# Modulation scale summed on TensorE, shift on VectorE, and the first products taken channel tile by channel tile

## The chip, the cores and the metric

The kernel runs on one core of one Trainium2 chip. The time is that of the device, in microseconds (us), for one launch; the kernel before was run three times, and its median is 2421.31 us. Engines are named as in the profile: PE (TensorE's matmuls), PEld (its weight loads), DVE (VectorE), ACT (ScalarE), POOL (GpSimd) and SP (SyncE, which issues most DMAs).

## The reference

Two transformer blocks on 1024 tokens with 1024 channels. The change lies in the first: a condition vector is turned into shift, scale and gate, the normalised x is modulated by the first two, and a gated delta net (8 key heads, 16 value heads, chunks of 64 tokens) runs on the result.

```
cond = silu(c)
mod = cond @ ada_w[0] + ada_b[0]                       # 1024 -> 3 * 1024
shift, scale, gate = split(mod, 3)
hdn = rms_norm(x, norm_g) * (1.0 + scale) + shift
proj = hdn @ w_in                                      # q, k, v, z, b_lin, a_lin
qkv = silu(causal_depthwise_conv(qkv, conv_w))         # 4 taps
beta = sigmoid(b_lin)
g = -exp(a_log) * softplus(a_lin + dt_bias);  gc = cumsum(g) in each chunk
... delta rule, chunk by chunk: y
x = x + gate * y;  x = rms_norm(x, final_g)
```

The second block (window attention, latent attention and a layer of 16 experts) is not touched.

## The kernel before

All matrices are fp32. A product is made of three matmuls in a reduced fp32 format: each operand is split into a high part (`hi`, a copy by ACT) and a low part (`lo`, the difference, by DVE), and `mm3` adds hi x hi, hi x lo and lo x hi in PSUM (L691 to L693). A matmul takes a weight tile of 128x128 and 512 tokens; a projection of 128 channels (`project`) is 8 channel tiles x 2 halves of the tokens x 3 = 48 matmuls into a PSUM tile of 128x1024 (`psj`). Two such tiles exist (pool `pj`), and they take turns: the third product can start only when the first tile has been read out.

The order of the first block:

- `norm_in` loads x in 8 tiles of 128 tokens (SP's queue). For four tiles at a time, ACT takes the sums of squares (L152), DVE the inverse root in eleven small steps (L154, L34 to L40), ACT normalises (L158), PE transposes (L161, eight 128x128 pieces a tile), and ACT copies into `xT` (L162): channels on partitions, tokens along a row.
- Meanwhile `ada_w` comes in blocks of 128x1024 (512 KB each) through six buffers. `matvec` multiplies each by a column of `cond` and adds it up on DVE (L134, L136), the 8 blocks of the scale first, then the 8 of the shift; PE takes the sums over the partitions against a column of ones (L167), and DVE finishes `mod` and `sc` (L190, L191).
- `modulate` works on halves of 512 tokens: ACT writes `hThi` (L175), DVE and POOL take turns in scaling `xT` in place (L179, L177), and DVE writes `hTlo` (L180).
- `decay` makes the product for beta and g (weights `wbh`, `wbl`), copies it out (`ba`, L239), and goes through a chain of small steps on DVE, ACT and PE (`pba`, `pcs`, `pcr`) to `gr` (L292), which SP stores to DRAM (`gc_d`) and loads again spread out (`D`).
- `gdn` projects K (`yk`), then makes the gate vector in `ada_gate`, with 8 more blocks of `ada_w` (three buffers, SP's queue, behind the store of `gr`), summed on DVE in `accg` and over the partitions on PE (L204); then Q (`yq`), the first two V heads (`yv`), and so on for 8 key heads. `conv_silu` reads a product with ACT (first tap, L221) and DVE (the other three taps, L224), which frees its PSUM tile.

Which instruction follows which on an engine is set by a scheduler from the order of the code; each engine then works through its own list in order, and waits on semaphores for the others. The names that the rows below use: `accg` is the gate's sum, `psm` and `psg` the PSUM tiles of the vectors' partition sums, `pgr` and `ptk` those of the first small products of a key head.

Of the kernel before, what the change touches and what calls it, by code (L numbers as in the profile page):

```python
# [10 lines left out]
F32 = mybir.dt.float32  # L11
# [35 lines left out]
class Net:  # L47
# [20 lines left out]
    def block1(self):  # L68
        nc, a = self.nc, self.a
        with ExitStack() as ps_, ExitStack() as big:  # L70
            self.gc_st = ExitStack()
            self.gc_pool = self.pool(self.gc_st, "g_c", "right")
            pa = self.pool(ps_, "pa", space=PSUM)
            pj = self.pool(big, "pj", "right", PSUM)
            hp = self.pool(big, "hp", "right")
            self.wp = self.pool(big, "g_w", "right")
            hT = [[hp.tile([128, T], F32R, name=f"{n}{k}") for k in range(KT)] for n in ("hThi", "hTlo")]
            with ExitStack() as s0:
                dk = self.pool(s0, "dk", "right")
# [3 lines left out]
                self.decay(hT, pj, pa, dk)  # L83
# [44 lines left out]
    def matvec(self, p, col, acc, bufs, tag="adaw"):  # L128
        nc = self.nc
        for k in range(KT):  # L130
            w = p.tile([128, 1024], F32, tag=tag, name="adaw", bufs=bufs)
            nc.sync.dma_start(w, self.a["ada_w"][0, k * 128:k * 128 + 128, col:col + 1024])
            if k == 0:
                nc.vector.tensor_scalar(acc, w, self.cond[:, 0:1], None, op0=OP.mult)  # L134
            else:
                nc.vector.scalar_tensor_tensor(acc, w, self.cond[:, k:k + 1], acc, op0=OP.mult, op1=OP.add)  # L136

    def norm_in(self, pj, pa, hT, p):
        nc, a = self.nc, self.a
        ident = self.ident  # L140
        acc = [p.tile([128, 1024], F32, name=f"acc{i}") for i in range(2)]
# [5 lines left out]
        sc = p.tile([128, KT], F32, name="sc")  # L147

        def norm(h):
            tiles = range(h * 4, h * 4 + 4)  # L150
            for t in tiles:
                nc.scalar.activation(jk, xs[t], AF.Square, accum_out=ss[:, 0, t:t + 1])  # L152
            s = slice(h * 4, h * 4 + 4)
            nc.vector.tensor_scalar(ss[:, 0, s], ss[:, 0, s], 1.0 / D, EPS, op0=OP.mult, op1=OP.add)  # L154
            rsqrt(nc, p, ss[:, 1, s], ss[:, 0, s], [4])
            for t in tiles:
                x = xs[t]
                nc.scalar.activation(x, x, AF.Copy, scale=ss[:, 1, t:t + 1])  # L158
                pt = pj.tile([128, KT, 128], F32, tag="pj", name="pt", bufs=2)
                for k in range(KT):  # L160
                    nc.tensor.transpose(pt[:, k], x[:, k * 128:(k + 1) * 128], ident)  # L161
                nc.scalar.activation(xT[:, :, t * 128:(t + 1) * 128], pt, AF.Copy)  # L162

        def modulation(i):
            self.matvec(p, i * 1024, acc[i], 6)
            for m in range(8):
                nc.tensor.matmul(ps[:, i * 8 + m:i * 8 + m + 1], lhsT=acc[i][:, m * 128:m * 128 + 128],  # L167
                                 rhs=self.ones[:, 0:1], start=True, stop=True)

        def modulate(h):  # L170
            s = slice(h * 512, h * 512 + 512)
            for k in range(KT):
                sh, sg = mod[:, k:k + 1], sc[:, k:k + 1]
                hi, lo, x = hT[0][k][:, s], hT[1][k][:, s], xT[:, k, s]
                nc.scalar.activation(hi, x, AF.Identity, bias=sh, scale=sg)  # L175
                if k % 2:
                    nc.gpsimd.tensor_scalar(x, x, sg, sh, op0=OP.mult, op1=OP.add)  # L177
                else:
# [12 lines left out]
        nc.vector.scalar_tensor_tensor(sc, mod[:, 8:16], 1.0, self.ngain, op0=OP.add, op1=OP.mult)  # L191
        modulate(0)
        modulate(1)

    def ada_gate(self, pa, p):
        nc, a = self.nc, self.a
        acc = p.tile([128, 1024], F32, tag="y_q", name="accg", bufs=2)
        self.matvec(p, 2048, acc, 3, "y_vz")
        row = p.tile([1, D], F32, tag="y_q", name="grow", bufs=2)
        nc.gpsimd.dma_start(row, a["ada_b"][:, 2048:3072])  # L200
# [27 lines left out]
    def decay(self, hT, pj, pa, q):  # L228
        nc = self.nc
        p = self.gc_pool  # L230
        hi, lo = self.wba
        self.split(hi[:, :, 0:32], lo[:, :, 0:32], self.wbf)
        ps = pj.tile([128, T], F32, tag="pj", name="psj", bufs=2)
        for n in range(2):
            for k in range(KT):
                s = slice(n * 512, (n + 1) * 512)
                self.mm3(ps[:, s], hi[:, k], lo[:, k], hT[0][k][:, s], hT[1][k][:, s], k == 0, k == KT - 1)
# [19 lines left out]
        s = q.tile(S3, F32, name="s")  # L257
# [1354 lines left out]
```

## Time and profile before

| | us |
|---|---|
| runs | 2420.91, 2421.31 (median), 2424.42 |
| profiled execution | 2423.83, of it span 2422.1 |
| PE busy | 2302.6 (95%) |
| DVE busy | 1840.0 (76%) |
| ACT busy | 1387.7 (57%) |
| POOL busy | 160.4 (7%) |

PE is the busiest engine by far. The page's picture of 40 slices of 60 us gives the first of them busy shares of 5 and 8 tenths for PE and nearly all others 9, so what PE can still save lies at the start and in a few slices near 1850 us. The rows further below are from the first 140 us, and one from a later stretch.

### The profile page before, as it was taken

The page shows a single profiled execution, that of the slowest core. Times are in us where ns is not written, and L with a number is a line of the kernel's source. Part 1 is how long each engine was busy: PE and PEld are TensorE (multiplying, and loading weights), DVE is VectorE, ACT ScalarE, POOL GpSimd, SP SyncE. Part 2 cuts the span into 40 slices and gives each one's busy share as a digit, 9 for nine tenths or more (in the row PEclk, how much of TensorE's full clock was granted, in tenths as well). Part 3 has the DMA queues.
Part 4 walks back from the last instruction along what each step waited for, and adds up shares of the span by engine and source line. Part 5 has one row for each costly group of instructions (what it writes and reads, how often), then busy time and mean ns, then how long its engine had stood idle before and what let it go on. Part 6 is the DMA issues. An engine that isn't in the chain of part 4 may idle for free. (4 is left out here: it accounts for less than half of the span.)

```text
span 2422.1 us, 34804 instructions
## 1 busy us (share of the span) xinstructions
PE 2302.6 (95%) x12285; PEld 1884.2 (78%) x12285; DVE 1840.0 (76%) x4307; ACT 1387.7 (57%) x2505; POOL 160.4 (7%) x254
## 2 busy tenths in 40 slices
PE   5899999999999999999999999999976999999998
PEld 4678788888878776777887887887865888888886
DVE  6896778595867854475448978886897898988986
ACT  6344545463544433342437767776434777777775
POOL 2100100001000000000000000000001111111110
PEclk8999999999999999999999989999997999999999
DMA  6422331223222134574412222103347999999993
GB/s 230 147 64 49 79 79 43 77 53 79 62 66 75 32 87 157 171 214 135 76 43 62 72 72 76 30 14 120 119 161 272 370 392 379 385 391 371 381 385 108
DMA packets 262905, 373.99 MB, mean 154 GB/s; under 512 B 90785, under 2 KB 179745, under 8 KB 262730
## 3 DMA queue, kind: packets, MB, share of 16 engines
q1 hardware_dynamic: 217450, 322.51, 39.5%
q10 hardware_dynamic: 39504, 28.15, 4.0%
q0 software_dynamic: 5776, 21.11, 3.2%
q8 instruction: 97, 1.59, 0.3%
q14 instruction: 78, 0.64, 0.1%
HBM read 327.53 MB, written 44.18 MB: 153 GB/s over the span
## 5 line engine op out<-in xcount | busy, mean ns | idle before, releaser
L53 DVE TENSOR_TENSOR whl<-wf,whl 128x2048 fp32r<-128x2048 f32 (+1 forms) x195 | 436.5, 2256 | 55.7 <-ACT whl L52 53.9
L52 ACT ACTIVATE whl<-wf 128x2048 fp32r<-128x2048 f32 (+1 forms) x195 | 368.8, 1895 | 106.4 <-PE psg L693 103.1
L693 PE MATMUL psj<-hThi,wlo 128*128 128x512 f32 x768 | 316.8, 413 | 0.0
L691 PE MATMUL psj<-hThi,whi 128*128 128x512 f32 x768 | 316.5, 412 | 0.0
L692 PE MATMUL psj<-hTlo,whi 128*128 128x512 f32 x768 | 315.4, 411 | 0.0
L692 PE MATMUL psg<-whl,th 128*128 128x512 f32 x768 | 305.1, 397 | 0.0
L693 PE MATMUL psg<-whl,tl 128*128 128x512 f32 x768 | 303.5, 395 | 1.0 <-DVE tl L53 1.0
L691 PE MATMUL psg<-whl,th 128*128 128x512 f32 x768 | 295.5, 400 | 0.0
L52 ACT ACTIVATE whi<-wf 128x512 fp32r<-128x512 f32 (+1 forms) x112 | 77.1, 691 | 184.9 <-PE psj L692 153.4
L693 PEld LDWEIGHTS psg<-whl,tl 128*128 128x128 f32 x768 | 144.9, 189 | 34.5 <-DVE tl L53 1.4
L692 PEld LDWEIGHTS psg<-whl,th 128*128 128x128 f32 x768 | 145.1, 189 | 34.1 <-DVE whl L53 1.6
L691 PEld LDWEIGHTS psg<-whl,th 128*128 128x128 f32 x768 | 144.5, 189 | 32.7 <-ACT th L52 0.6
L692 PEld LDWEIGHTS psj<-hTlo,whi 128*128 128x128 f32 x768 | 146.0, 190 | 24.8
L693 PEld LDWEIGHTS psj<-hThi,wlo 128*128 128x128 f32 x768 | 146.0, 190 | 24.5 <-issue 0.2
L691 PEld LDWEIGHTS psj<-hThi,whi 128*128 128x128 f32 x768 | 145.7, 190 | 24.2
L53 DVE TENSOR_TENSOR wlo<-wf,whi 128x512 fp32r<-128x512 f32 (+1 forms) x112 | 85.1, 762 | 88.8 <-ACT whi L52 87.3
L691 PE MATMUL psy<-whi,ohi 128*128 128x512 f32 x240 | 96.4, 402 | 7.2 <-ACT ohi L52 7.2
L52 ACT ACTIVATE th<-pst 128x512 fp32r<-128x512 f32 x110 | 59.4, 567 | 71.4 <-PE pst L836 42.0
L693 PE MATMUL psy<-whi,olo 128*128 128x512 f32 x240 | 96.4, 402 | 3.6 <-DVE olo L53 3.5
L53 DVE TENSOR_TENSOR pl<-psP,ph 128x512 fp32r<-128x512 f32 x128 | 82.7, 683 | 20.4 <-ACT ph L52 19.4
L692 PE MATMUL psy<-wlo,ohi 128*128 128x512 f32 x240 | 95.7, 399 | 0.0
L52 ACT ACTIVATE ph<-psP 128x512 fp32r<-128x512 f32 x128 | 69.4, 594 | 32.5 <-PE psP L1141 28.5
(447 smaller groups left out, 5196.2 us busy)
## 6 DMA issues: line engine op xcount, KB each, us to landing
wf<-in_w_down_dram SPq DMA_DIRECT2D x64, 1024.0 KB, 7.4
wf<-in_w_gate_dram SPq DMA_DIRECT2D x62, 1024.0 KB, 8.7
wf<-in_w_up_dram SPq DMA_DIRECT2D x62, 1024.0 KB, 9.1
wf<-in_gdn_w_in_dram SPq DMA_DIRECT2D x96, 256.0 KB, 3.0
of<-oT_d ACTq DMA_DIRECT2D x60, 256.0 KB, 3.4
adaw<-in_ada_w_dram SPq DMA_DIRECT2D x24, 512.0 KB, 5.2
D<-gc_d SPq DMA_DIRECT2D x32, 256.0 KB, 3.2
oT_d<-z SPq DMA_DIRECT2D x16, 512.0 KB, 3.0
```

The lines of the kernel that those rows point to most:

```text
L52: self.halved = (self.nc.scalar.activation(hi, src, AF.Copy), self.nc.vector.tensor_sub(lo, src, hi.bitcast(F32)))
L53: self.nc.vector.tensor_sub(lo, src, hi.bitcast(F32)))
L691: nc.tensor.matmul(ps, lhsT=ah, rhs=wh, start=first, stop=False)
L692: nc.tensor.matmul(ps, lhsT=ah, rhs=wl, start=False, stop=False)
L693: nc.tensor.matmul(ps, lhsT=al, rhs=wh, start=False, stop=last)
```

## The change

Four things change in the first block.

- **Vectors.** The blocks of shift and scale come in turn (shift 0, scale 0, shift 1, ...), through seven buffers; the first of each is issued by GpSimd, the others by SP. The shift is summed by DVE as before; for the scale PE multiplies each piece of 128x128 of a block with its column of `cond` (N = 1, 64 products), and DVE adds up the 8 partial sums. The small loads are issued before the norms.
- **Modulation.** It goes by channel tile, all 1024 tokens at once. ACT scales `xT` for tiles 2, 4 and 6, DVE for the others; POOL does nothing here.
- **First products.** `first_products` makes the decay product and the first K product together, channel tile by channel tile, in the two PSUM tiles; `decay` starts from the finished product, and the first `conv_in("k")` takes the finished K.
- **Gate.** The partition sums of `accg` are 8 products with N = 1 into a column, in place of two with N = 512 into a row, and the bias is loaded and the result stored as a column, 4 bytes at a time.

```diff
@@ norm_in
-        def modulation(i):
-            self.matvec(p, i * 1024, acc[i], 6)
-            for m in range(8):
-                nc.tensor.matmul(ps[:, i * 8 + m:i * 8 + m + 1], lhsT=acc[i][:, m * 128:m * 128 + 128],
-                                 rhs=self.ones[:, 0:1], start=True, stop=True)
...
-        def modulate(h):
-            s = slice(h * 512, h * 512 + 512)
-            for k in range(KT):
-                sh, sg = mod[:, k:k + 1], sc[:, k:k + 1]
-                hi, lo, x = hT[0][k][:, s], hT[1][k][:, s], xT[:, k, s]
-                nc.scalar.activation(hi, x, AF.Identity, bias=sh, scale=sg)
-                if k % 2:
-                    nc.gpsimd.tensor_scalar(x, x, sg, sh, op0=OP.mult, op1=OP.add)
-                else:
-                    nc.vector.tensor_scalar(x, x, sg, sh, op0=OP.mult, op1=OP.add)
-                nc.vector.tensor_sub(lo, x, hi.bitcast(F32))
+        def modulate(k):
+            sh, sg = mod[:, k:k + 1], sc[:, k:k + 1]
+            hi, lo, x = hT[0][k], hT[1][k], xT[:, k]
+            nc.scalar.activation(hi, x, AF.Identity, bias=sh, scale=sg)
+            if k in (2, 4, 6):
+                nc.scalar.activation(x, x, AF.Identity, bias=sh, scale=sg)
+            else:
+                nc.vector.tensor_scalar(x, x, sg, sh, op0=OP.mult, op1=OP.add)
+            nc.vector.tensor_sub(lo, x, hi.bitcast(F32))
...
+        blocks = []
+        for k in range(KT):
+            for i in range(2):
+                blocks.append(self.ada_block(p, i * 1024, k, 7, eng=nc.gpsimd if k == 0 else None))
+        self.small_loads()
         norm(0)
-        modulation(1)
-        modulation(0)
-        self.small_loads()
         norm(1)
-        nc.vector.tensor_add(mod, ps[:, 0:16], self.adab)
+        for k in range(KT):
+            self.matvec(blocks[2 * k], k, acc)
+            for m in range(8):
+                nc.tensor.matmul(part[:, m, k:k + 1], lhsT=blocks[2 * k + 1][:, m * 128:m * 128 + 128],
+                                 rhs=self.cond[:, k:k + 1], start=True, stop=True)
+        self.column_sums(ps[:, 0:8], acc)
+        nc.vector.tensor_reduce(mod[:, 8:16], part, axis=AX.X, op=OP.add)
+        nc.vector.tensor_add(mod[:, 8:16], mod[:, 8:16], self.adab[:, 8:16])
         nc.vector.scalar_tensor_tensor(sc, mod[:, 8:16], 1.0, self.ngain, op0=OP.add, op1=OP.mult)
-        modulate(0)
-        modulate(1)
+        nc.vector.tensor_add(mod[:, 0:8], ps[:, 0:8], self.adab[:, 0:8])
+        for k in range(KT):
+            modulate(k)
@@ ada_gate
-        for n in range(2):
-            s = slice(n * 512, n * 512 + 512)
-            ps = pa.tile([128, 512], F32, tag="a", name="psg", bufs=2)
-            nc.tensor.matmul(ps, lhsT=self.ones, rhs=acc[:, s], start=True, stop=True)
-            nc.vector.tensor_add(row[:, s], row[:, s], ps[0:1])
-        nc.sync.dma_start(self.gate_d, row)
+        col = p.tile([128, 8], F32, tag="gcol", name="gcol")
+        nc.sync.dma_start(col, a["ada_b"][:, 2048:3072].rearrange("o (m p) -> p (o m)", p=128))
+        ps = pa.tile([128, 512], F32, tag="a", name="psg", bufs=2)
+        self.column_sums(ps, acc)
+        nc.vector.tensor_add(col, col, ps[:, 0:8])
+        nc.sync.dma_start(self.gate_d.rearrange("o (m p) -> p (o m)", p=128), col)
+    def first_products(self, hT, pj):
+        hi, lo = self.wba
+        self.split(hi[:, :, 0:32], lo[:, :, 0:32], self.wbf)
+        psd, psk = [pj.tile([128, T], F32, tag="pj", name="psj", bufs=2) for i in range(2)]
+        w = [self.load_w(self.wp, self.w_in[:, kk:kk + 4, 1024:1152], [4, 128], bufs=3) for kk in (0, 4)]
+        for k in range(KT):
+            for ps, wh, wl in ((psd, hi[:, k], lo[:, k]), (psk, w[k // 4][0][:, k % 4], w[k // 4][1][:, k % 4])):
+                for n in range(2):
+                    s = slice(n * 512, (n + 1) * 512)
+                    self.mm3(ps[:, s], wh, wl, hT[0][k][:, s], hT[1][k][:, s], k == 0, k == KT - 1)
+        return psd, psk
```

How the lists of the engines move. First PE, from the fourth transposed tile of x to the first product, in the kernel before (`pt` is a tile in transposition, `psm` the vectors' sums):

```order
L161 MATMUL pt_208<-ident_67,x3_143 128x128 x8
L167 MATMUL psm_138<-ones_116,acc1_133 128x1 x8
L161 MATMUL pt_308<-ident_67,x4_144 128x128 x8
L161 MATMUL pt_319<-ident_67,x5_145 128x128 x8
L161 MATMUL pt_330<-ident_67,x6_146 128x128 x8
L161 MATMUL pt_341<-ident_67,x7_147 128x128 x8
L167 MATMUL psm_138<-ones_116,acc0_132 128x1 x8
L691 MATMUL psj_404<-hThi0_87,wbh_123 128x512
```

The four transposed tiles of the second half stand together, between the two sets of column sums. The same place on PE after the change, from the fifth tile of x (`x4`) on:

```order
L168 MATMUL pt_275<-ident_67,x4_143 128x128 x8
L194 MATMUL psm_137<-cond_106,adaw_173 128x1 x7
L168 MATMUL pt_286<-ident_67,x5_144 128x128 x8
L194 MATMUL psm_137<-cond_106,adaw_173 128x1
L168 MATMUL pt_297<-ident_67,x6_145 128x128 x8
L194 MATMUL psm_137<-cond_106,adaw_177 128x1 x8
L168 MATMUL pt_308<-ident_67,x7_146 128x128 x8
L194 MATMUL psm_137<-cond_106,adaw_181 128x1 x8
L194 MATMUL psm_137<-cond_106,adaw_185 128x1 x8
L142 MATMUL psm_137<-ones_116,acc_132 128x1 x8
L705 MATMUL psj_429<-hThi0_87,wbh_123 128x512
```

Products of four blocks of the scale (`adaw_173` to `adaw_185`) now stand among and behind the transposes, and the shift's column sums behind them. Second, PE around `pba`, the first small step of the decay chain on PE, in the kernel before (`wbh`, `wbl` are the decay weights, `whi`, `wlo` those of K):

```order
L691 MATMUL psj<-hThi_94,wbh 128x512
L692 MATMUL psj<-hTlo_102,wbh 128x512
L693 MATMUL psj<-hThi_94,wbl 128x512
L693 MATMUL psj<-hThi_87,wlo 128x512
L691 MATMUL psj<-hThi_87,whi 128x512
L692 MATMUL psj<-hTlo_95,whi 128x512
L693 MATMUL psj<-hThi_87,wlo 128x512
L691 MATMUL psj<-hThi_88,whi 128x512
L242 MATMUL pba<-ident,ba 128x32 x8
```

Here the decay product ends when K has just begun (`hThi_87` and `hThi_94` are the first and the last channel tile). The same place after the change:

```order
L706 MATMUL psj<-hTlo_102,wbh 128x512
L707 MATMUL psj<-hThi_94,wbl 128x512
L705 MATMUL psj<-hThi_94,whi 128x512
L706 MATMUL psj<-hTlo_102,whi 128x512
L707 MATMUL psj<-hThi_94,wlo 128x512
L705 MATMUL psj<-hThi_94,whi 128x512
L706 MATMUL psj<-hTlo_102,whi 128x512
L707 MATMUL psj<-hThi_94,wlo 128x512
L255 MATMUL pba<-ident,ba 128x32 x8
```

The decay product now ends six matmuls before the end of K, and the matmuls behind `pba` are those of Q. Third, DVE from `gr` to the third tap of K after the change (`accg` is the first step on the gate's first block):

```order
L305 COPY gr<-pcr 128x128
L299 TENSOR_TENSOR kdf<-kdf,beta 128x128
L53 TENSOR_TENSOR wlo<-wf,whi 128x512
L244 SCALAR_TENSOR_TENSOR yk<-psj,cw,yk 128x1023
L244 SCALAR_TENSOR_TENSOR yk<-psj,cw,yk 128x1022
L136 TENSOR_SCALAR accg<-adaw,cond 128x1024
L244 SCALAR_TENSOR_TENSOR yk<-psj,cw,yk 128x1021
```

This list reads as before but for its line numbers: the gate's first step stands between the second and the third tap of K.

## Rows read from the trace of the kernel before

**Rows 1.** Windows: busy us of PE, PEld, DVE, ACT, POOL; PEclk; DMA share; GB/s.
```profile
8.00:12.00 4.00, 0.00 (x0) 0.00 (x0) 0.00 (x0) 3.12 (x5) 0.00 (x0) 1.00 1.04 392
...
32.00:36.00 4.00, 3.75 (x18) 3.75 (x19) 3.83 (x7) 3.23 (x3) 0.00 (x0) 0.50 0.88 321
36.00:40.00 4.00, 3.92 (x24) 3.68 (x22) 3.89 (x4) 1.94 (x2) 0.00 (x0) 0.67 0.99 296
...
48.00:52.00 4.00, 4.00 (x10) 2.53 (x10) 3.97 (x7) 4.00 (x6) 3.94 (x3) 0.50 0.00 0
...
sum 140.00, PE 103.61 PEld 81.14 DVE 105.90 ACT 76.36 POOL 24.50; mean PE 2.96 PEld 2.32 DVE 3.03 ACT 2.18 POOL 0.70
...
180.00:220.00 40.00, 40.00 (x294) 33.53 (x293) 21.96 (x71) 17.09 (x58) 5.43 (x20) 1.00 0.24 52
```

**Rows 2.** Timeline, ACT: start, duration, line, operation, [idle before <-releaser].
```profile
11.18 1.06 ACT L152 ACTIVATE jk<-x 128x1024 f32<-128x1024 f32 x1 [0.20 <-DMA x<-in_x_dram]
...
14.74 4.27 ACT L158 ACTIVATE x<-x,ss 128x1024 f32<-128x1024 f32 x4 [1.11 <-DVE ss L40]
...
24.85 1.06 ACT L152 ACTIVATE jk<-x 128x1024 f32<-128x1024 f32 x1
...
32.70 3.23 ACT L158 ACTIVATE x<-x,ss 128x1024 f32<-128x1024 f32 x3 [6.70 <-DVE ss L40]
...
45.02 11.41 ACT L175 ACTIVATE hThi<-xT,mod,sc 128x512 fp32r<-128x512 f32 x16 [1.26 <-DVE sc L191]
...
65.67 1.02 ACT L239 ACTIVATE ba<-psj 32x1024 f32<-32x1024 f32 x1 [7.68 <-PE psj L693]
```

**Rows 3.** Timeline, DVE, from the second inverse root to `sc`.
```profile
26.03 0.17 DVE L154 TENSOR_SCALAR ss<-ss 128x4 f32<-128x4 f32 x1 [2.19 <-ACT jk L152]
...
33.36 9.21 DVE L136 SCALAR_TENSOR_TENSOR acc<-adaw,cond,acc 128x1024 f32<-128x1024 f32 x7
...
44.82 0.17 DVE L191 SCALAR_TENSOR_TENSOR sc<-mod,ng 128x8 f32<-128x8 f32 x1
```

**Rows 4.** Timeline, PE, before the first product.
```profile
32.25 3.57 PE L167 MATMUL psm<-ones,acc 128*128 128x1 f32 x16 [9.57 <-DVE acc L136]
35.69 4.23 PE L161 MATMUL pt<-ident,x 128*128 128x128 f32 x24
...
42.62 1.95 PE L167 MATMUL psm<-ones,acc 128*128 128x1 f32 x16 [0.34 <-DVE acc L136]
```

**Rows 5.** Timeline, DVE, first and last steps of the modulation.
```profile
45.87 0.55 DVE L179 TENSOR_SCALAR xT<-xT,sc,mod 128x512 f32<-128x512 f32 x1 [0.88 <-ACT hThi L175]
...
62.86 1.27 DVE L180 TENSOR_TENSOR hTlo<-xT,hThi 128x512 fp32r<-128x512 f32 x2
```

**Rows 6.** Timeline, PE, from the end of the modulation to V1.
```profile
64.19 0.50 PE L692 MATMUL psj<-hTlo,wbh 128*128 128x512 f32 x1 [2.04 <-DVE hTlo L180]
...
77.92 0.39 PE L691 MATMUL psj<-hThi,whi 128*128 128x512 f32 x1
...
88.82 0.39 PE L691 MATMUL psj<-hThi,whi 128*128 128x512 f32 x1
...
99.13 1.98 PE L204 MATMUL psg<-accg,ones 128*128 128x512 f32 x4 [0.85 <-DVE accg L136]
...
109.31 0.77 PE L691 MATMUL psj<-hThi,whi 128*128 128x512 f32 x1
```

**Rows 7.** Timeline, DVE, from `gr` to the gate's last block.
```profile
77.89 0.28 DVE L292 COPY gr<-pcr 128x128 f32<-128x128 f32 x1
...
83.75 0.75 DVE L134 TENSOR_SCALAR accg<-adaw,cond 128x1024 f32<-128x1024 f32 x1 [1.46 <-DMA adaw<-in_ada_w_dram]
84.42 1.28 DVE L224 SCALAR_TENSOR_TENSOR yk<-psj,cw,yk 128x1021 f32<-128x1021 f32 x1
...
97.79 1.29 DVE L136 SCALAR_TENSOR_TENSOR accg<-adaw,cond,accg 128x1024 f32<-128x1024 f32 x1
```

More of the change, by code (lines that the diff above doesn't have):

```diff
@@ L82, in block1 @@
                     self.norm_in(pj, pa, hT, self.pool(s1, "n1"))
-                self.decay(hT, pj, pa, dk)
+                psd, self.psk = self.first_products(hT, pj)
+                self.decay(psd, pa, dk)
             with ExitStack() as s2:
@@ L126, in small_loads, with ada_block, matvec, column_sums @@
         nc.sync.dma_start(self.nw, a["gdn_norm_w"].rearrange("o (p u) -> (o p) u", u=1))
-    def matvec(self, p, col, acc, bufs, tag="adaw"):
-        nc = self.nc
-        for k in range(KT):
[L131 to L134, printed above, removed]
-            else:
-                nc.vector.scalar_tensor_tensor(acc, w, self.cond[:, k:k + 1], acc, op0=OP.mult, op1=OP.add)
+    def ada_block(self, p, col, k, bufs, tag="adaw", eng=None):
+        w = p.tile([128, 1024], F32, tag=tag, name="adaw", bufs=bufs)
+        (eng or self.nc.sync).dma_start(w, self.a["ada_w"][0, k * 128:k * 128 + 128, col:col + 1024])
+        return w
+    def matvec(self, w, k, acc):
+        if k == 0:
+            self.nc.vector.tensor_scalar(acc, w, self.cond[:, 0:1], None, op0=OP.mult)
+        else:
+            self.nc.vector.scalar_tensor_tensor(acc, w, self.cond[:, k:k + 1], acc, op0=OP.mult, op1=OP.add)
+    def column_sums(self, ps, acc):
+        for m in range(8):
+            self.nc.tensor.matmul(ps[:, m:m + 1], lhsT=acc[:, m * 128:m * 128 + 128], rhs=self.ones[:, 0:1], start=True, stop=True)
     def norm_in(self, pj, pa, hT, p):
@@ L140, in norm_in @@
         ident = self.ident
-        acc = [p.tile([128, 1024], F32, name=f"acc{i}") for i in range(2)]
+        acc = p.tile([128, 1024], F32, name="acc")
         jk = p.tile([128, D], F32, name="jk")
@@ L147, in norm_in @@
         sc = p.tile([128, KT], F32, name="sc")
+        part = ps[:, 64:128].rearrange("p (m k) -> p m k", k=KT)
         def norm(h):
@@ L162, in norm @@
                 nc.scalar.activation(xT[:, :, t * 128:(t + 1) * 128], pt, AF.Copy)
-        def modulation(i):
-            self.matvec(p, i * 1024, acc[i], 6)
-            for m in range(8):
-                nc.tensor.matmul(ps[:, i * 8 + m:i * 8 + m + 1], lhsT=acc[i][:, m * 128:m * 128 + 128],
-                                 rhs=self.ones[:, 0:1], start=True, stop=True)
-        def modulate(h):
-            s = slice(h * 512, h * 512 + 512)
-            for k in range(KT):
-                sh, sg = mod[:, k:k + 1], sc[:, k:k + 1]
-                hi, lo, x = hT[0][k][:, s], hT[1][k][:, s], xT[:, k, s]
-                nc.scalar.activation(hi, x, AF.Identity, bias=sh, scale=sg)
-                if k % 2:
-                    nc.gpsimd.tensor_scalar(x, x, sg, sh, op0=OP.mult, op1=OP.add)
-                else:
-                    nc.vector.tensor_scalar(x, x, sg, sh, op0=OP.mult, op1=OP.add)
-                nc.vector.tensor_sub(lo, x, hi.bitcast(F32))
+        def modulate(k):
[4 more added lines that the diff above has]
+                nc.scalar.activation(x, x, AF.Identity, bias=sh, scale=sg)
+            else:
+                nc.vector.tensor_scalar(x, x, sg, sh, op0=OP.mult, op1=OP.add)
+            nc.vector.tensor_sub(lo, x, hi.bitcast(F32))
         xs = [p.tile([128, D], F32, name=f"x{t}") for t in range(NT)]
@@ L184, in norm_in @@
             nc.sync.dma_start(xs[t], a["x"][0, t * 128:(t + 1) * 128, :])
+        blocks = []
[3 more added lines that the diff above has]
+        self.small_loads()
         norm(0)
-        modulation(1)
-        modulation(0)
-        self.small_loads()
         norm(1)
-        nc.vector.tensor_add(mod, ps[:, 0:16], self.adab)
+        for k in range(KT):
+            self.matvec(blocks[2 * k], k, acc)
+            for m in range(8):
+                nc.tensor.matmul(part[:, m, k:k + 1], lhsT=blocks[2 * k + 1][:, m * 128:m * 128 + 128],
[3 more added lines that the diff above has]
+        nc.vector.tensor_add(mod[:, 8:16], mod[:, 8:16], self.adab[:, 8:16])
         nc.vector.scalar_tensor_tensor(sc, mod[:, 8:16], 1.0, self.ngain, op0=OP.add, op1=OP.mult)
-        modulate(0)
-        modulate(1)
+        nc.vector.tensor_add(mod[:, 0:8], ps[:, 0:8], self.adab[:, 0:8])
+        for k in range(KT):
+            modulate(k)
     def ada_gate(self, pa, p):
@@ L197, in ada_gate @@
         acc = p.tile([128, 1024], F32, tag="y_q", name="accg", bufs=2)
-        self.matvec(p, 2048, acc, 3, "y_vz")
-        row = p.tile([1, D], F32, tag="y_q", name="grow", bufs=2)
-        nc.gpsimd.dma_start(row, a["ada_b"][:, 2048:3072])
-        for n in range(2):
-            s = slice(n * 512, n * 512 + 512)
-            ps = pa.tile([128, 512], F32, tag="a", name="psg", bufs=2)
-            nc.tensor.matmul(ps, lhsT=self.ones, rhs=acc[:, s], start=True, stop=True)
-            nc.vector.tensor_add(row[:, s], row[:, s], ps[0:1])
-        nc.sync.dma_start(self.gate_d, row)
+        for k in range(KT):
+            self.matvec(self.ada_block(p, 2048, k, 3, "y_vz"), k, acc)
+        col = p.tile([128, 8], F32, tag="gcol", name="gcol")
[9 more added lines that the diff above has]
+        w = [self.load_w(self.wp, self.w_in[:, kk:kk + 4, 1024:1152], [4, 128], bufs=3) for kk in (0, 4)]
+        for k in range(KT):
+            for ps, wh, wl in ((psd, hi[:, k], lo[:, k]), (psk, w[k // 4][0][:, k % 4], w[k // 4][1][:, k % 4])):
[3 more added lines that the diff above has]
+        return psd, psk
     def project(self, pj, hT, src):
@@ L226, in conv_silu, with decay @@
         nc.scalar.activation(y, y, AF.Silu)
-    def decay(self, hT, pj, pa, q):
+    def decay(self, ps, pa, q):
         nc = self.nc
         p = self.gc_pool
[L231 to L237, printed above, removed]
         ba = q.tile([32, T], F32, name="ba")
@@ L303, in gdn @@
         ng = getattr(self, "ng", 8)
-        kT = self.conv_in("k", 1024)
+        kT = self.conv_in("k", 1024, ps=self.psk)
         self.ada_gate(pa, p)
@@ L341, in oload_early, with conv_in @@
         return {i: (hi[:, i], lo[:, i]) for i in range(4)}
-    def conv_in(self, nm, col, tag=None, bufs=2):
-        ps = self.project(self.pj, self.hT, self.w_in[:, :, col:col + 128])
+    def conv_in(self, nm, col, tag=None, bufs=2, ps=None):
+        if ps is None:
+            ps = self.project(self.pj, self.hT, self.w_in[:, :, col:col + 128])
         y = self.gp.tile([128, T], F32, tag="y_" + (tag or nm), name="y" + nm, bufs=bufs)
```

## The prediction

> **What bounds the kernel now.** I read the busy time by stretches of 40 us first. From 180 us on PE works 40.00 of 40.00 us at full clock [rows 1]. Nearly all later stretches look like it, so a shift of the moment at which PE becomes saturated is carried to the end, one for one. The change touches only what lies before that: the first 140 us, in which PE is busy for 103.61 us and idle for 36.4 [rows 1]. There the question is what PE waits for. The timeline of the single engines shows it: ACT waits for x to land, DVE sums the modulation vectors, PE transposes, and all of it meets in `sc`, ready at 44.82 + 0.17 = 44.99 us, from which the modulation starts [rows 2 to 4]. I call this moment t0, and the same moment in the changed kernel t0'. A second meeting point lies behind it: PE starts the second V product (V1) at 109.31, t0 + 64.3, after a column of waits that begins with the decay product [rows 6, 7]. So the working has two parts: how far t0 moves, and how far V1 moves against t0.
>
> The profiled execution took 2423.83 us (span 2422.1 and 1.7 around it), 2.5 above the median of the runs, 2421.31. I sum against 2423.83 and take 2.5 off at the end.
>
> **Part 1: the two norms, the vectors, and t0.**
> *Loads.* Two blocks of 512 KB now go out on GpSimd's queue while x is loading. The transfers already move 392 GB/s in that stretch at a DMA share of 1.04 [rows 1], so each block costs whatever shares the engines with it 512 KB / 392 GB/s = 1.34 us. The fourth x tile is needed first: its square begins 0.20 us after it lands, at 11.18 [rows 2]. Bounds of its delay: 0 (the blocks come behind x) and 2.7 us (both ahead of it). I take 2.5, since the second queue starts at the same time as SP's. Then the first normalisation moves from 14.74 to 17.2, and the ACT chain behind it, with the last square (24.85 + 1.06), ends at 28.4 instead of 25.9. The Trainium skill, "DMA: Bandwidth & Descriptors", section "Issuing engines are not separate DMA queues", says that transfers started from sync, scalar and gpsimd run on the same 16 engines and interleave, and that a second issuer saves only issue time. By that rule the delay is real and near 2.7; were the queues apart, it would be 0.
>
> *The second rsqrt.* From 26.03 to 32.70 its eleven small steps took 6.7 us [rows 2, 3], because DVE put a matvec step of about 1.2 us between them four times. With the scale's eight blocks off DVE, one or two come between: 6.7 less 2.4 to 3.6. The second normalisation then starts at 28.5 + 3.1 to 4.3, so at 31.6 to 32.8; I take 32.7, no gain. Without the DMA delay it would be 30.2.
>
> *PE between the norms and t0.* Here the change costs. Its order is strict: four transposed tiles (8 passes each), with the scale's blocks 4 to 7 between and behind them, then the shift's column sums. An fp32 product with one column appears as two passes (16 records for 8 products, rows 4). So behind the second normalisation PE has 4 x 8 + 4 x 16 + 16 = 112 passes, against 32 + 16 before, and before the first 24 transposes already ran while DVE still summed. At the low clock a pass costs (35.69 - 32.25)/16 = 0.215 us, at the high one 1.95/16 = 0.122 [rows 4]. From 33.8 (first tile normalised) that is 24.1 or 13.7 us, to 57.9 or 47.5. Add 0.8 for the reduction and the small sums (four steps of 0.2; t0's own two took 0.4, rows 3): t0' = 58.7 or 48.3. DVE's 9.21 us of seven matvec steps, which set t0 before, would no longer be the bound: eight shift steps are done when the loads are, 24 x 1.34 us after about 5, near 37.
>
> *Which clock.* The 16 one-column passes at 32.25 left PE at a granted clock of 0.50, the 1.2 GHz level, through 32 to 36; the clock rose only within 36 to 40 (mean 0.67: two thirds at 0.50, so at about 38.6), after three microseconds of transposes in one piece [rows 1, 4]. In the changed order no such piece exists: bursts of 8 transposes stand between runs of one-column products. So I take the low clock for most of it, and a rise late among the last blocks: **t0' = 56, +11**. Bounds: 45.5 (no DMA delay, high clock: 31.0 + 13.7 + 0.8) and 59.
>
> **Part 2: from t0' to V1.**
> *Modulation.* Before, DVE ended at 62.86 + 1.27 = 64.13, 19.1 us after t0 [rows 5]. Now DVE has five scalings of 128x1024 at 0.75 (the same form, rows 7) and eight subtractions at two of 128x512, 1.27 [rows 5]: 13.9, and 0.9 until ACT's first high part (the idle time in rows 5). ACT has eleven at 4.27/4 = 1.07 [rows 2], 11.8. So 15 us, a gain of 4.
>
> *Two products interleaved.* PE takes decay and K tile by tile, 96 matmuls at 0.2275 (Q's 48 lie between 77.92 and 88.82, rows 6). Some 25 are out when the fifth tile's low part comes, t0' + 11.3; the other 71 take 16.2: done at t0' + 27.5. K thus ends 5.4 us earlier than before (Q followed it at 77.92, t0 + 32.9). But the decay sum is complete only as the 90th of the 96, at t0' + 26.1. Before, ACT read it at 65.67, t0 + 20.7 [rows 2]. The chain behind it is unchanged and took 65.67 to 77.89 + 0.28 = 78.17, 12.5 us; since its two small products wait on PE behind 39 matmuls of Q, I count 13.6. Its end, `gr`, moves from t0 + 33.2 to **t0' + 39.7**.
>
> *What hangs on gr.* The store of gr stands on SP ahead of the gate's blocks, so the first block landed 83.75 - 78.17 = 5.6 us after it [rows 7]; now, with a weight load between, 6.3: t0' + 46.0. On DVE that block's step stands ahead of the third tap of yk (84.42, rows 7), and PE's V0 needs the PSUM buffer that this tap frees. V0 began at 88.82, t0 + 43.8; there Q had only just ended, so the wait cost nothing. Now PE is through Q at t0' + 27.5 + 0.9 + 48 x 0.2275 + about 1 = t0' + 40.2, and the tap ends at 46.0 + 0.75 + 1.28 = t0' + 48.0: a **new stall of 8 us**, which takes all that the shorter modulation gained, and 4.3 more. After it the clock is low for some 3 us (as in 48 to 52 after an idle stretch, rows 1), and V0 ends near t0' + 62.
>
> *To V1.* The gate's last block step began at 97.79, 14.0 after the first; t0' + 46.0 + 14.0 + 1.3 gives 61.3, no earlier than V0's end. The column sums then take 16 passes, 1.9, in place of the 1.98 at 99.13 [rows 6, 7]: nothing. The four transposes of yk and the two rows of small products before V1 wait for ACT as before. V1 starts near t0' + 67.7 against t0 + 64.3: +3.4; some of the transposes and small products stand inside V1 now, some five at a matmul's 0.2275, +1.2. **Part 2: +4.6.** Bounds: 0 (the stall eats only idle time that PE had anyway, some 2.0 us at 64.19 among it, rows 6) and +7 (the wait counts in full, with the low clock behind it). I take the middle since the chain is counted step by step.
>
> The gate's 4-byte column load and store, instead of one row, lie behind V1 and far ahead of their use, hidden by the saturated PE; were they late, it would show only as a wait in the output stage.
>
> **Sum.** 11 + 4.6 = +15.6: 2423.83 + 15.6 = 2439.4, less 2.5: 2437.
>
> **Rivals.**
> - *The clock holds.* The transposes may be enough to raise it, as the 24 did at 38.6 [rows 1, 4]. Then t0' = 48.3, +3.3, and with part 2 +7.9: 2429; with an earlier second norm and a smaller part 2 down to 2422. Against it: the run at 32.25.
> - *The gate chain is not the bound: faster.* The place is the third tap of yk. If the first gate block lands before Q is through (t0' + 40), the stall of 8 us does not appear. Then PE runs the 192 matmuls of decay, K, Q and V0 nearly in one piece: 27.5 + 1.9 + 2 x 10.9 = t0' + 51 for V0's end instead of t0 + 54.8, and V1 starts about 6 earlier against t0'. With t0' = 45.5 that is -5.5: 2416. It decides from gr + 6.3 under t0' + 40, so it needs a decay sum ready 6 us sooner than its place as the 90th matmul allows. The shorter modulation and K's earlier end speak for it.
> - *The change does not do what it says:* the scale's blocks come so late that PE waits for the loads. The stream of 24 blocks ends near 37, and the last products follow within 4 us, so t0' would be near t0; with part 2, +5: 2426.
>
> **How the numbers follow.** Low clock with the stall: 0.60, its own range 2430 to 2444. The clock holds: 0.25, of which a third within the bound of no change. Faster: 0.10. Late loads: 0.05. The measurement tells 0.2%, 4.8 us, from no change: under 2416.5 counts as faster, over 2426.1 as slower. Faster: 0.10 less what falls within the bound, 0.08. Same: 0.02 + 0.08 + 0.04 + a remainder, 0.16. Slower: 0.76. The range, 2420 to 2445, leaves out the faster rival and the cold end above 59.
>
> **What would show it.** Right: PE's clock at 0.50 between about 30 and 55 us; the one-column passes as a line with some 25 us on PE; `sc` near 56; ACT's read of the decay sum near t0' + 26; a wait of several us on PE at V0's first matmul, released by DVE's yk; from 180 us on the old pattern, moved by about 15. Wrong: a clock of 1.00 among the one-column products, `sc` before 46, or V0 following Q without a gap.

## The result and the profile after

The changed kernel took 2440.85 us (median of 4 runs, 2437.01 to 2444.12), against 2422.77 for the kernel before in the same comparison: a ratio of 1.0076, interval 1.0064 to 1.0089. It is slower by 18 us; 2437 had been forecast, as the likeliest of four cases. The two profiled executions differ by 2438.3 - 2422.1 = 16.2 us of span, and the traces show where they arise.

The windows of the changed kernel, with the columns of [rows 1]:

```profile
24.00:28.00 4.00, 4.00 (x36) 4.00 (x34) 1.28 (x1) 3.93 (x6) 0.00 (x0) 0.91 1.04 425
28.00:32.00 4.00, 4.00 (x21) 4.00 (x20) 3.39 (x14) 0.52 (x3) 0.00 (x0) 0.50 1.03 410
...
36.00:40.00 4.00, 4.00 (x20) 4.00 (x21) 2.40 (x2) 0.50 (x1) 0.00 (x0) 0.50 0.99 287
40.00:44.00 4.00, 4.00 (x35) 4.00 (x34) 0.17 (x1) 2.56 (x4) 0.00 (x0) 0.89 0.71 192
44.00:48.00 4.00, 4.00 (x22) 4.00 (x22) 0.00 (x0) 1.25 (x2) 0.00 (x0) 0.54 0.10 27
48.00:52.00 4.00, 4.00 (x21) 4.00 (x20) 0.00 (x0) 0.00 (x0) 0.00 (x0) 0.50 0.00 0
...
96.00:100.00 4.00, 0.00 (x0) 0.00 (x0) 2.87 (x3) 1.58 (x2) 0.00 (x0) 0.87 0.62 198
100.00:104.00 4.00, 1.26 (x3) 1.10 (x4) 3.35 (x4) 1.32 (x2) 0.00 (x0) 0.50 0.95 341
...
180.00:220.00 40.00, 40.00 (x255) 33.81 (x254) 24.54 (x46) 10.86 (x19) 5.90 (x19) 1.00 0.34 72
```

From 44 to 52 us PE is busy without a pause, at half the clock, while DVE, ACT and the transfers do next to nothing: all of the kernel waits for PE. From 96 to 100 it is the reverse, PE does nothing at all. From 180 us on PE is full again, as in [rows 1], so what was lost by then stays lost.

The timeline of PE:

```profile
24.75 7.96 PE L194 MATMUL psm<-cond,adaw 128*128 128x1 f32 x48
32.91 1.97 PE L168 MATMUL pt<-ident,x 128*128 128x128 f32 x8 [0.20 <-ACT x L165]
34.68 2.98 PE L194 MATMUL psm<-cond,adaw 128*128 128x1 f32 x14
...
41.10 1.84 PE L194 MATMUL psm<-cond,adaw 128*128 128x1 f32 x16
...
43.72 6.28 PE L194 MATMUL psm<-cond,adaw 128*128 128x1 f32 x32
49.86 3.55 PE L142 MATMUL psm<-ones,acc 128*128 128x1 f32 x16
...
82.24 0.68 PE L255 MATMUL pba<-ident,ba 32*128 32x32 f32 x8
...
102.74 0.76 PE L705 MATMUL psj<-hThi,whi 128*128 128x512 f32 x1 [7.65 <-DVE yk L244]
...
117.75 2.04 PE L142 MATMUL psg<-ones,accg 128*128 128x1 f32 x16 [2.45 <-DVE accg L138]
...
123.08 0.80 PE L705 MATMUL psj<-hThi,whi 128*128 128x512 f32 x1
```

It answers to [rows 4, 6]. The column sums end at 49.86 + 3.55 = 53.41, where those before ended at 44.57; V0 begins at 102.74 after a wait of 7.65 us, where it followed Q without one; V1 begins at 123.08 instead of 109.31.

DVE and ACT, to be held against [rows 2, 3, 5, 7]:

```profile
53.91 0.17 DVE L199 SCALAR_TENSOR_TENSOR sc<-mod,ng 128x8 f32<-128x8 f32 x1
...
66.49 2.36 DVE L179 TENSOR_TENSOR hTlo<-xT,hThi 128x1024 fp32r<-128x1024 f32 x2
...
93.98 0.29 DVE L305 COPY gr<-pcr 128x128 f32<-128x128 f32 x1
...
100.65 0.75 DVE L136 TENSOR_SCALAR accg<-adaw,cond 128x1024 f32<-128x1024 f32 x1 [1.43 <-DMA adaw<-in_ada_w_dram]
101.31 1.28 DVE L244 SCALAR_TENSOR_TENSOR yk<-psj,cw,yk 128x1021 f32<-128x1021 f32 x1
...
116.32 1.28 DVE L138 SCALAR_TENSOR_TENSOR accg<-adaw,cond,accg 128x1024 f32<-128x1024 f32 x1 [1.15 <-DMA adaw<-in_ada_w_dram]
```

```profile
13.35 1.06 ACT L159 ACTIVATE jk<-x 128x1024 f32<-128x1024 f32 x1 [1.24 <-DMA x<-in_x_dram]
...
16.92 4.27 ACT L165 ACTIVATE x<-x,ss 128x1024 f32<-128x1024 f32 x4 [1.08 <-DVE ss L40]
...
31.71 3.23 ACT L165 ACTIVATE x<-x,ss 128x1024 f32<-128x1024 f32 x3 [3.48 <-DVE ss L40]
...
80.98 1.02 ACT L252 ACTIVATE ba<-psj 32x1024 f32<-32x1024 f32 x1 [5.59 <-PE psj L707]
```

So t0' = 53.91 + 0.17 = 54.08, and the shift is +9.1 at `sc`, +13.8 at V1 and +16.2 at the end. It does not grow evenly on the way: at the taps of the V products behind V1 it lies between 9.4 and 19.7; gate_column, below, shows which part of the change does that.

### The profile page after: what moved, and what is told of

The parts are those of the page before. It is cut to its first block, busy times and chain, and to the rows that moved or that the text cites. A ratio compares the mean times of both kernels' runs of the same rounds, so it can differ in the third digit from the quotient of the medians.

```text
span 2438.3 us, 35024 instructions
## 1 busy us (share of the span) xinstructions
PE 2321.6 (95%) x12409; PEld 1903.6 (78%) x12409; DVE 1830.9 (75%) x4289; ACT 1388.8 (57%) x2500; POOL 147.4 (6%) x247
## 5 line engine op out<-in xcount | busy, mean ns | idle before, releaser
L705 PEld LDWEIGHTS psg<-whl,th 128*128 128x128 f32 x768 | 144.5, 189 | 32.8 <-ACT th L52 0.6
```

Of the source, the lines that this page charges most:

```text
L705: nc.tensor.matmul(ps, lhsT=ah, rhs=wh, start=first, stop=False)
```

## The experiments

Ten kernels were run. The first table gives, for the profiled execution of each, where some steps begin, as a difference to the kernel before (us; `V1 tap` is ACT's first tap on V1's product, `last tap` that of the sixteenth value head). It tells in which stage a kernel gains or loses; the second gives the times, with the ratio and its 95% interval as they are on record (the ratio is not the quotient of the two medians).

| | sc | gr | V1 tap | last tap | span |
|---|---|---|---|---|---|
| before (start, us) | 44.8 | 77.9 | 124.0 | 849.8 | 2422.1 |
| changed | +9.1 | +16.1 | +13.8 | +15.5 | +16.2 |
| scale_on_dve | +0.9 | +7.9 | +7.1 | +7.8 | +2.0 |
| decay_first | +8.9 | +6.0 | +3.5 | +5.4 | +7.4 |
| gate_on_gpsimd | +12.3 | +19.2 | +12.1 | +26.9 | +27.1 |
| both_undone | +1.4 | -1.6 | -3.9 | -1.9 | -6.7 |
| scale_behind | +13.6 | +20.8 | +19.8 | +20.6 | +23.1 |
| tiles_only | -0.3 | -3.3 | -4.3 | -3.6 | -4.2 |
| tiles_ng | +1.5 | -1.5 | +3.1 | +1.7 | +3.5 |
| tiles_gate_late | -0.2 | -3.1 | -8.0 | -5.4 | -5.0 |
| tiles_scale_part | +3.3 | +0.3 | +0.9 | +1.2 | -1.9 |
| gate_column | 0.0 | +1.5 | -0.3 | +1.2 | -2.8 |

| | median us | before, beside it | ratio | interval |
|---|---|---|---|---|
| scale_on_dve | 2426.58 | 2423.37 | 1.0016 | 1.0007 to 1.0025 |
| decay_first | 2429.08 | 2423.37 | 1.0023 | 1.0014 to 1.0032 |
| gate_on_gpsimd | 2447.79 | 2423.37 | 1.0094 | 1.0081 to 1.0108 |
| both_undone | 2416.99 | 2423.37 | 0.9972 | 0.9956 to 0.9988 |
| scale_behind | 2443.08 | 2425.96 | 1.0078 | 1.0055 to 1.0102 |
| tiles_only | 2419.47 | 2425.96 | 0.9985 | 0.9972 to 0.9999 |
| tiles_ng | 2418.30 | 2425.96 | 0.9978 | 0.9965 to 0.9990 |
| tiles_gate_late | 2418.93 | 2425.96 | 0.9975 | 0.9962 to 0.9989 |
| tiles_scale_part | 2419.24 | 2421.97 | 0.9988 | 0.9979 to 0.9996 |
| gate_column | 2420.43 | 2421.97 | 0.9991 | 0.9982 to 0.9999 |

Each row of the first table is one execution, and it need not be a typical one: that of tiles_ng took 2427.39 us, the longest of 12. Behind the last tap, where no edit reaches, the lag still moves by -5.8 us (scale_on_dve) to +2.5 us (scale_behind). So a few us of a span or a time can't be laid to one early stage; the columns up to V1 are the ones to argue from.

**scale_on_dve.**

```diff
-            self.matvec(blocks[2 * k], k, acc)
-            for m in range(8):
-                nc.tensor.matmul(part[:, m, k:k + 1], lhsT=blocks[2 * k + 1][...], rhs=self.cond[:, k:k + 1], ...)
+            for i in range(2):
+                self.matvec(blocks[2 * k + i], k, acc[i])
...
+        for i in range(2):
+            self.column_sums(ps[:, i * 8:i * 8 + 8], acc[i])
```

> The changed kernel with the scale summed on DVE again, like the shift (blocks still in turn, six buffers, both column sums at the end); the rest as changed. My account: PE's 112 one-column passes and transposes at the low clock set sc; without them sc is ready at 45 to 48 us instead of 54.1, and the whole time falls by 6 to 9 us, to about 2433, no further, since the stall before V0 stays. Rival (the late sc comes from the loads: GpSimd's two blocks and the alternation): sc stays above 51 and the time within 3 us of 2441.

`sc` began at 45.7, 8.2 us earlier than in the changed kernel, and up to the last tap 7.7 us of that remained. The rival is out: the loads were the same (the fourth x tile's square at 13.32 and 13.35), and late `sc` went with PE's products. The wait at V0 stayed (8.09). The median fell by 14, twice what was expected; 6.5 us of that arise behind the last tap (-7.7 there, -14.2 at the end, against the changed kernel), in stages that the edit does not touch, and stay unexplained. PE before `sc`, and at V0:

```profile
35.98 3.50 PE L167 MATMUL pt<-ident,x 128*128 128x128 f32 x16 [11.88 <-ACT x L164]
40.01 2.00 PE L167 MATMUL pt<-ident,x 128*128 128x128 f32 x16 [0.53 <-ACT xT L168]
41.85 3.63 PE L142 MATMUL psm<-ones,acc 128*128 128x1 f32 x32
...
95.01 0.76 PE L701 MATMUL psj<-hThi,whi 128*128 128x512 f32 x1 [8.09 <-DVE yk L240]
```

Behind 32 transposes in one piece, 32 one-column passes took 3.63 us, 0.113 each; in the changed kernel 32 of them took 6.28 (at 43.72), 0.196 each.

**decay_first.**

```diff
-                psd, self.psk = self.first_products(hT, pj)
+                psd, self.psk = self.first_products(hT, pj), None
...
-        for k in range(KT):
-            for ps, wh, wl in ((psd, ...), (psk, ...)):
+        for k in range(KT):          # psd alone; conv_in("k") projects K behind decay
```

> The changed kernel with the decay product made first and K's product behind the decay chain's start, as before (still by channel tile); vectors, modulation and gate as changed. My account: the decay sum comes some 9 us earlier against sc, the wait of 7.65 us at V0's first matmul shrinks to under 2 us, and the time falls by 5 to 8 us, to about 2434; sc stays at 54. Rival (the wait comes from the slower gate loads or from the changed gate itself): the wait at V0 stays above 5 us and the time within 3 us of 2441.

With `sc` where it was (+8.9), `gr` came 10 us earlier than in the changed kernel, and the wait at V0 is not only smaller but gone: in the list of PE's waits from 53 to 130 us (what waits, for what, us in total, times, longest) no `yk` of DVE stands.

```profile
PE ptk L377 <- ACT jk L378: 2.7, 2, 2.0
PE psj L703 <- POOL V L312: 2.1, 1, 2.1
PE psj L704 <- DVE hTlo L179: 1.3, 1, 1.3
PE psj L705 <- DVE wlo L53: 0.4, 1, 0.4
PE pcs L285 <- issue: 0.3, 1, 0.3
```

V1 came 10.3 us earlier, the median 11.8. That is more than 5 to 8: against `sc`, V1 is now 5.4 us earlier than in the kernel before (3.5 - 8.9), so the shorter modulation pays once the interleaving does not eat it.

**gate_on_gpsimd.**

```diff
-            self.matvec(self.ada_block(p, 2048, k, 3, "y_vz"), k, acc)
+            self.matvec(self.ada_block(p, 2048, k, 3, "y_vz", eng=nc.gpsimd), k, acc)
```

> The changed kernel with the gate's eight blocks issued by GpSimd's queue instead of SP's, so that they no longer stand behind the store of gr; all else as changed. My account: the first block is there long before the K taps, DVE's list lets the third tap pass, PE goes from Q to V0 with under 2 us of wait, and the time falls by 4 to 7 us, to about 2436, though gr is as late as before. Rival (gr's lateness itself binds, through D and the first key head): the wait moves to a later place and the time stays within 3 us of 2441.

My account failed: the time rose by 7 us, to 2447.79, and the wait at V0 was 8.41, though the first blocks were issued at 73.88, over 20 us ahead of `gr`. The rival's cause held (D, and with it `gr`), but not its outcome: the wait did not move to a later place, and the time left the 3 us around 2441. DVE, and PE at V0 and V1:

```profile
99.77 2.60 DVE L244 SCALAR_TENSOR_TENSOR yk<-psj,cw,yk 128x1023 f32<-128x1023 f32 x2 [0.31 <-ACT yk L241]
104.97 0.35 DVE L394 SCALAR_TENSOR_TENSOR D<-D,gc,maskU 128x128 f32<-128x128 f32 x1 [2.60 <-DMA D<-gc_d]
105.24 1.27 DVE L244 SCALAR_TENSOR_TENSOR yk<-psj,cw,yk 128x1021 f32<-128x1021 f32 x1
```

```profile
106.66 0.76 PE L705 MATMUL psj<-hThi,whi 128*128 128x512 f32 x1 [8.41 <-DVE yk L244]
...
121.00 0.47 PE L705 MATMUL psj<-hThi,whi 128*128 128x512 f32 x1 [0.76 <-DVE yq L244]
```

Where the gate's first step had stood ahead of the third tap, a step on `D` stands now, and `D` is read back from the store of `gr`. So for the wait at V0 the gate's load was only the messenger: what binds there is `gr`, through whichever of its followers stands ahead of the third tap in DVE's list. A list in which the tap stands ahead of them all was not tried. Behind V0 the gate's steps do count: V1 began at 121.00, 2.1 us earlier than in the changed kernel, although 3.2 us more were lost at `sc`, where the clock stayed low for one burst longer. Later the gate's steps lie among those of the next heads, and the last tap is 11 us later than in the changed kernel.

**both_undone** is scale_on_dve and decay_first in one.

> Scale on DVE and decay first together; what is left of the change is the modulation by channel tile, the alternating loads with two on GpSimd, and the gate's column. If the two parts are independent, the gains add: 2441 - 8 - 7 = 2426, between 2421 and 2430; the modulation's 4 us show as an earlier end of DVE's lo steps against sc (15 us instead of 19). If one hides the other, the time stays at 2431 or more.

2416.99, below the 2421 to 2430 that I had given, because each of the two parts had turned out larger than forecast. Measured one by one they gained 14.3 and 11.8 us, 26.1 together; in one kernel they gain 23.9, so they very nearly add. This version is faster than both kernels. DVE's last low part ended 14.8 us after `sc` (61.12 against 46.35).

**scale_behind.**

```diff
+        cond2 = p.tile([128, KT], F32, name="cond2")
+        nc.vector.scalar_tensor_tensor(cond2, xT[:, :, T - 1], 0.0, self.cond, op0=OP.mult, op1=OP.add)
...
-                                 rhs=self.cond[:, k:k + 1], start=True, stop=True)
+                                 rhs=(cond2 if k > 3 else self.cond)[:, k:k + 1], start=True, stop=True)
```

> The changed kernel, but the scale's products of blocks 4 to 7 take their column from a copy of cond that is made after the last transposed tile, so that all 32 transposes of the second half stand in one piece on PE and 64 one-column products' passes plus the column sums come behind. The same work, later. If the low clock is what makes the passes slow (0.215 us against 0.113 to 0.122): the transposes raise the clock to 1.00, the 80 passes behind run at least at first at the high rate, and sc is ready at 49 to 53 us in spite of the later start, at 54.1 at the latest. If a pass is slow for another reason, the 80 passes take 17 us from about 40.5 on, and sc comes at 58.

`sc` came at 58.4, the rival's time, but not for the rival's reason. PE, and the windows:

```profile
34.40 4.36 PE L168 MATMUL pt<-ident,x 128*128 128x128 f32 x24
40.03 1.09 PE L168 MATMUL pt<-ident,x 128*128 128x128 f32 x8 [1.28 <-ACT x L165]
42.44 12.06 PE L196 MATMUL psm<-cond,adaw 128*128 128x1 f32 x64 [1.32 <-DVE cond L192]
```

```profile
36.00:40.00 4.00, 2.75 (x18) 2.52 (x16) 1.28 (x1) 3.11 (x4) 0.00 (x0) 0.80 0.90 288
40.00:44.00 4.00, 2.65 (x22) 2.42 (x23) 1.36 (x2) 2.30 (x3) 0.00 (x0) 1.00 0.60 146
44.00:48.00 4.00, 4.00 (x23) 4.00 (x22) 0.00 (x0) 0.00 (x0) 0.00 (x0) 0.55 0.49 137
```

The transposes in one piece did raise the clock, to 1.00 between 40 and 44 us, and the products began at that rate. But at about 44.4 (a tenth of the window from 44 on) the clock fell in the midst of a run of one-column products without a gap. So they are slow through the clock, as I held; that they would profit much from a clock raised ahead of them was wrong, since it fell while they ran. PE had stood idle for 1.32 us ahead of them, but the idle time is not needed for the fall: in the changed kernel the run of 48 passes at 24.75 follows the transposes without a gap, and the clock went from 0.91 (24 to 28 us) to 0.50 (28 to 32 us) while PE was busy throughout.

**tiles_only** takes the kernel before and changes the modulation alone; decay's loops run channel tile by channel tile, the order of the products stays.

```diff
-        modulate(0)
-        modulate(1)
+        for k in range(KT):
+            modulate(k)          # as in the change
...
-        for n in range(2):
-            for k in range(KT):
+        for k in range(KT):
+            for n in range(2):   # decay product
```

> The kernel before with one part of the change alone: the modulation by channel tile (ACT scaling tiles 2, 4 and 6, POOL none) and the decay product taken tile by tile, ahead of K as before. Vectors, loads and gate as before. My account: sc stays at 45.0, DVE's last lo step ends 15 us after sc instead of 19, gr comes 3 to 4 us earlier, and the time falls by 3 to 6 us against before, to about 2418. Rival (what both_undone gained came from the loads in turn or the gate's column): no gain, within 1.5 us of before.

DVE:

```profile
44.54 0.17 DVE L189 SCALAR_TENSOR_TENSOR sc<-mod,ng 128x8 f32<-128x8 f32 x1
...
57.13 2.36 DVE L178 TENSOR_TENSOR hTlo<-xT,hThi 128x1024 fp32r<-128x1024 f32 x2
```

The last low part ended 14.8 us after `sc`, as expected. `sc` as before, `gr` 3.3 us and V1 4.3 us earlier, and the span 4.2 shorter. The rival is out by these instants: this part of the change is a gain by itself. The time alone would not exclude it, since the interval (0.9972 to 0.9999) reaches to within 0.3 us of no gain.

**tiles_ng.**

```diff
-        nc.scalar.dma_start(self.adab, ...)
+        nc.gpsimd.dma_start(self.adab, ...)
...
-        nc.scalar.dma_start(self.ngain, ...)
+        nc.gpsimd.dma_start(self.ngain, ...)
```

> As tiles_only, with the two loads of 4-byte elements that ACT issues at the start (ng and adab) issued by GpSimd instead. In both kernels the seventh load of x leaves SP only when such a load has landed (12.50 before, 16.16 changed). If that wait costs time, the loads of x and of the vectors' blocks come 1 to 4 us earlier, sc comes 0.5 to 2 us earlier, and the time falls by as much against tiles_only. If DVE's matvec steps alone set sc, it stays at 45.0 and nothing is gained.

SP issued its eight loads of x within 4.56 us:

```profile
1.64 4.56 SPq L182 DMA_DIRECT2D x<-in_x_dram  x8
```

(12.41 in tiles_only.) But `sc` came 1.8 us later, not earlier, and the intervals of the two ratios overlap: the early issue bought nothing. Neither forecast fits, for `sc` did not stay either. ACT waited 1.90 us for the second x tile, whose square began at 9.41 against 7.96 in tiles_only, and the first normalisation began 1.2 us later (15.48 for 14.24); DVE's last seven steps began 0.9 us later (34.01 for 33.09), and the column sums behind them took 2.78 us for 1.95. Why that tile landed later was not tested.

**tiles_gate_late.**

```diff
-        self.ada_gate(pa, p)
...
         for g in range(ng):
+            if g == 2:
+                self.ada_gate(pa, p)
```

> As tiles_only, with the gate's eight matvec steps and sums moved from ahead of the first key head to ahead of the third, where PE is saturated and DVE has room. My account: DVE loses 10 us of work between 80 and 103 us, V0 and V1 follow without the waits for accg and the late taps, V1 starts 4 to 7 us earlier than in tiles_only, and the time falls by 3 to 7 us more, to about 2413. Rival (the buffers that the gate's blocks borrow from the heads, or DVE's work later, stall PE there): the gain at V1 is given back by the fourth head, and the time is that of tiles_only or above.

V1 came 3.7 us earlier than in tiles_only, and the next K 6.2; by the last tap 1.8 were left, and in the times nothing can be told (2418.93 for 2419.47). My 3 to 7 us were wrong. The rival's outcome held: the gain was given back among the later heads; which of its two causes did it was not looked into.

**tiles_scale_part** sends the scale's blocks 0 and 1 to PE and the other fourteen to DVE.

```diff
+            if part is not None and k < 2:
+                ...
+                for m in range(8):
+                    nc.tensor.matmul(part[:, m, k:k + 1], lhsT=w[:, m * 128:m * 128 + 128], rhs=self.cond[:, k:k + 1], ...)
+                continue
```

> As tiles_only, with only the first two of the scale's eight blocks summed on PE (N = 1, in the time in which PE waits for the second norm) and the other six, and the shift, on DVE; loads as before. My account: the scale on PE costs time only where its products stand between the second norm and sc; here none does, DVE is rid of two steps of 1.2 us, sc comes 1 to 2.4 us earlier than in tiles_only, and the time falls by as much, to about 2418 against 2419.5. Rival (DVE waits for the blocks to land anyway, or the products let PE's clock fall for the transposes): sc stays within 0.5 us or comes later, and nothing is gained.

`sc` came 3.6 us later than in tiles_only. PE:

```profile
20.10 1.92 PE L135 MATMUL psm<-cond,adaw 128*128 128x1 f32 x16 [0.88 <-DMA adaw<-in_ada_w_dram]
21.88 2.96 PE L170 MATMUL pt<-ident,x 128*128 128x128 f32 x16
...
34.37 3.57 PE L176 MATMUL psm<-ones,acc 128*128 128x1 f32 x16 [6.34 <-DVE acc L143]
37.81 5.36 PE L170 MATMUL pt<-ident,x 128*128 128x128 f32 x24
```

The first block's products stand ahead of the third transposed tile and wait there for their load; the transposes behind them, the ACT chain that waits for these, and with it the second inverse root came 2.4 us later than in tiles_only (28.14 for 25.71). Even two blocks were in the way, by their place in the list. The rival held: nothing was gained, in the time neither (2419.24 for 2419.47), where the 3.6 us lost at `sc` don't show.

**gate_column** is the kernel before with the change's `ada_gate`.

> The kernel before with the gate's change alone: partition sums as 8 one-column products, bias loaded and result stored as a column in 4-byte pieces. My account: 16 passes of 1.9 us in place of 1.98, the loads far off the path: the time of before within 2 us. Rival (the 4-byte transfers or the column's load in SP's queue delay the gate's blocks, D or the next weights): slower by 2 to 6 us.

2420.43 against 2421.97: within the 2 us, if anything to the good. In the time that part had rightly been put at nothing. In the trace it shifts the V products against each other: against the kernel before, the first tap on the sixth V product came 5.7 us earlier, the fifteenth 5.5 later, the last 1.2 later. The changed kernel jumps at the same taps (+9.4 and +19.7). Held against gate_column, and not against the kernel before, its lag is 14.2 us at V1's tap and 14.2 at the last: what was lost up to V1 was carried on one for one.

## Why the prediction was right

- *The loads.* The fourth x tile's square began at 13.35 instead of 11.18, +2.17, and the first normalisation at 16.92 (17.2 forecast). The two blocks on GpSimd's queue delayed x by most of their cost of 2.7. The Trainium skill, "DMA: Bandwidth & Descriptors", section "Issuing engines are not separate DMA queues", says that transfers started by the scalar, sync or gpsimd engine run on the same 16 DMA engines and interleave; the trace agrees, with 2.17 us where queues apart would have given 0.
- *The second rsqrt* ended for ACT at 31.71 (31.6 to 32.8): 1 us earlier than before, as the low end had it.
- *PE to t0.* 54.08 against 56: the stretch of 112 passes began at 32.91 instead of 33.8 and took 20.5 us instead of 21.4. The low clock came as forecast, with one burst at the high one (1.84 us for 16 passes at 41.10, the window's clock 0.89). I had placed the rise later, among the last blocks; it came earlier and was gone again for these (0.54 and 0.50 from 44 us on). scale_on_dve shows that this part is worth 8.2 of the 9.1 us.
- *Modulation.* 66.49 + 2.36 - 54.08 = 14.8 us (15 forecast); tiles_only shows the 4 us of gain alone.
- *Interleaved products.* ACT read the decay sum at t0' + 26.9 (26.1), `gr` was ready at t0' + 40.2 (39.7), the gate's first step began at t0' + 46.6 (46.0), the tap ended at t0' + 48.5 (48.0), and PE waited 7.65 us (8). decay_first removes this with all that hangs on it.
- *To V1: two terms mis-sized, one against the other.* "V1 starts near t0' + 67.7": it was 69.0, so +4.7 and not +3.4. The gate's last step began 15.7 us after the first, not 14.0; it ended at t0' + 63.5 and V0 at t0' + 61.2, where I had 61.3 and 62, so PE waited 2.45 us for it, a wait that I had put at nothing. The small products inside V1, put at +1.2, came to nothing in sum: from V1's start to its tap it took 14.8 us (137.85 - 123.08), and 14.7 in the kernel before (124.05 - 109.31). So part 2 was 4.7 up to V1's tap, against 4.6, by luck.
- *The sum: near by luck.* Part 1 was 1.9 too high, and the 2.4 us between V1's tap (+13.8) and the end (+16.2) stand nowhere in it; 15.6 against 16.2 comes of the two together. Of these 2.4, gate_column alone shows 1.5 (from -0.3 at V1's tap to +1.2 at the last); most of the rest (0.7) arises behind the last tap and stays unexplained.
- *What stood on a wrong link.* I named the gate's first block as what the tap waits for, and gave the faster rival its deciding point there. gate_on_gpsimd shows that without it DVE waits for `D` at the same place: the point was the lateness of `gr`, with DVE's list as the scheduler makes it.

Of the rivals, none came true. "The clock holds" was not met in the changed kernel, and scale_behind shows why not: one-column products did not hold it even where it had been raised (1.00, then 0.55 and 0.50). The times moved by 18.1, the spans by 16.2; the runs of the kernel before alone spread by more than the difference (2420.91 to 2424.42).

## What to carry to other kernels

Work moved to an idle engine is free only until the instant at which the old path ends: here PE was idle early, but the products that fell between the second norm and `sc` stood on the path, in PE's own order, at half the clock. Interleaving two products finishes the first nearly as late as the second (the decay product as the 90th of 96 matmuls); where a long chain of small steps hangs on one of them, that one goes first, and the other covers the chain. A change made of several parts is worth taking apart: the change with its two bad parts undone beat both kernels (0.28% faster than the kernel before), and so did, by a smaller margin that only just clears its interval, the modulation by tiles alone.

## What the runs showed of the hardware that was not expected

Products with one column, issued without a gap, did not keep the clock: in scale_behind it was 1.00 from 40 to 44 us and fell to 0.50 at about 44.4, within such a run, though PE's busy share was full; in the changed kernel it fell within the run that began at 24.75. From 48 to 52 us both kernels ran nothing but such products on PE, at 0.50. In scale_on_dve a run of 32 passes right behind the transposes was over (3.63 us) before it fell.
